# Weight panels fetched in pairs, and the quads of a fast matrix product regrouped for it

## The chip, the cores and the metric

The kernel runs on one core of a Trainium2 chip. A core has engines that work side by side, each through its own instructions in a fixed order: TensorE (PE, matrix products; PEld is its weight load), VectorE (DVE), ScalarE (ACT), GpSimd (POOL) and SyncE (SP), which here only issues DMA transfers. Engines wait for each other by semaphores. An instruction that waits holds up everything behind it on its engine. The metric is the device time of one execution, in microseconds (us).

## The reference

One step of a one-layer streaming encoder, in float32, for a prompt of 1024 rows and a sample of 64 rows, 1088 in all, with a model width of 1024. Cut to what matters:

```python
xn = rms_norm(x, g_pre)
z = xn @ w_in                    # 1024 -> 8208 columns, one projection for all that follows
xa, ga, q, k, v, gb, fl, ma, mb = jnp.split(z, np.cumsum(sizes)[:-1], axis=-1)
ua, conv_new = causal_conv(xa, conv_hist, conv_w, conv_b)
ya = rg_lru(ua, ...) * silu(ga)              # branch A, a gated linear recurrence
yb = fox_attention(q, k, v, logf) * silu(gb) # branch B, 16 heads of 64, causal, with forget gates
u = einsum('bsnw,nwd->bsnd', stack([ya, yb]), w_branch)
mix = sum(sigmoid(stack([ma, mb])) * u) @ w_o
h = x + rms_norm(mix, g_post)
h = h + rms_norm(sigmoid(h @ w_ple_gate) * (pe @ w_ple_proj), g_ple)
```

The keys, the values, the forget logits and the states are outputs too.

## The kernel before

Products keep float32 accuracy by splitting each operand into a high part (rounded) and a low part (what is left); three products, high x high, low x high and high x low, are summed. ScalarE writes the high part (`copy_act`, L82) and VectorE subtracts for the low part (`sub`, L85). So before a weight panel can be used, ScalarE reads it once ("wh") and VectorE once ("wl").

A *panel* is 128 columns of a weight matrix, 1024 x 128 numbers or 512 KB, in memory 1024 rows of 512 bytes. A plain panel takes 72 matmuls.

The stages, in order of time (us of the profile):

1. Norm and transposes of x, and the values v (to about 130), then two plain panels of a gate.
2. *Quads*, to about 431. A quad computes two panels at once by a fast product with seven instead of eight block products (`seven`). Each of the seven is 24 matmuls on one of three PSUM banks. Before the products, `split_pair` lets GpSimd form sums of the weight blocks (s1 to s4) and ScalarE and VectorE split them. While quad i runs, the weights of quad i + 1 are split and those of quad i + 2 fetched (`load_pair`). The eight first quads hold one key panel and one query panel each. Four others hold panels for branch A and for gates.
   Behind the products VectorE and ScalarE form sums of the banks (`u2`, `u3`, `p1`) and four results, by `put`: the first after the third product, then one each after the fifth, sixth and seventh. A key result is a tile "ko", a query result "qo", of which there are two buffers each. Results go to memory as a high part ("oh", by ScalarE's queue) and a low part ("kl" or "qo", by SP). Keys must also be transposed for the output: `keys_out` does this on TensorE ("tpk"), one item after each product (`between`), at the earliest three products after the result was made. A key buffer is free when the last of its items has run.
3. Attention, about 431 to 896. Its instruction order comes from a planner: the code runs through score, transpose and value steps in the order in which TensorE shall do them, counts their estimated durations (`spent`), and books the work of the other engines on a timetable (`book`, with costs as `D_MAX`, the row maximum on VectorE). Into this are mixed the matmuls of 18 plain panels (the gates), as `filler`, so that TensorE has work while the softmax runs. Loads of each head's q and k (`load_head`), the sample's data (`load_sample`) and the fillers' weights (`look_ahead`) are issued on SP in code order.
4. Branch A (to about 1068), the two products with w_branch ("a" to about 1182, "b" to about 1278), and the two last projections.

Weights for plain panels are fetched by `look_ahead` into two buffers of one panel each; `panel` and `book_split` split the next one while the present one is used. The order of instructions on each engine is fixed when the kernel is built; no engine picks another instruction when the first one waits.

Of the kernel before, what the change touches and what calls it, by code (L numbers as in the profile page):

```python
# [7 lines left out]
F32 = mybir.dt.float32  # L8
# [5 lines left out]
P = 128  # L14
D = 1024
KT = D // P
# [49 lines left out]
def hybrid_step(tc, a, o):  # L66
# [11 lines left out]
    def f(ap):  # L78
        return ap.bitcast(F32)

    def copy_act(out, in_, scale=1.0):
        act.activation(out=out, in_=in_, func=AF.Copy, scale=scale)  # L82

    def sub(eng, out, in0, in1):
        return eng.tensor_tensor(out=out, in0=in0, in1=in1, op=ALU.subtract)  # L85
# [106 lines left out]
    def chunk(steps):  # L192
        for _ in range(KT):
# [6 lines left out]


    wpool = sb("wpool", bufs=2)
    gates = deque([(w_in[:, c + k * P:c + (k + 1) * P], d[k]) for c, d in ((C_MA, d_ma), (C_MB, d_mb), (C_GB, d_gb))
                   for k in range(KT)])
    n_gates = len(gates)

    quads = [[(w_in[:, c + p * P:c + (p + 1) * P], (t, p)) for c, t in ((C_K, "k"), (C_Q, "q"))] for p in range(NP)]
    some = [(w_in[:, C_XA:C_XA + P], d_x0)]
    some += [(w_in[:, C_GA + k * P:C_GA + (k + 1) * P], d_ga[k]) for k in GA_EARLY]
    some += [gates.pop() for _ in range(2 * MORE)]  # L210
    quads += [[(src, ("r", dst)) for src, dst in some[i:i + 2]] for i in range(0, len(some), 2)]
# [5 lines left out]
    later = deque([(w_in[:, (C_XA if t == "x" else C_GA) + k * P:][:, :P], (t, k)) for t, k in branch_a]  # L217
                  + [(w_br[i * D:(i + 1) * D, k * P:(k + 1) * P], (t, k)) for i, t in enumerate("ab") for k in range(KT)])
    held_back = [True]
    ahead = deque()  # L220

    def choose():

        if held_back[0] and len(gates) <= n_gates - PLAIN:
            return None
        if gates:
            src, dst = gates.popleft()
            return src, ("r", dst)
        return later.popleft() if later else None

    def fetch(src, tag):
        raw = wpool.tile([P, KT, P], F32, name="wraw")
        tc.keep_in_program_order(sp.dma_start(raw[:, :, :], src.rearrange("(k p) n -> p k n", p=P)))
        ahead.append([tag, raw, None])

    def look_ahead():
        while len(ahead) < 2:
            nxt = choose()
            if nxt is None:
                return  # L240
            fetch(*nxt)

    def split_next(eng):
        if ahead and ahead[0][2] is None:
            raw = ahead[0][1]
            wh = wpool.tile([P, KT, P], F32R, name="wh")
            wl = wpool.tile([P, KT, P], F32R, name="wl")
            copy_act(wh[:, :, :], raw[:, :, :])
            sub(eng, wl[:, :, :], raw[:, :, :], f(wh[:, :, :]))
            ahead[0][2] = (wh, wl)  # L250

    def panel(eng=None):

        look_ahead()
        if not ahead:
            return None
        split_next(eng or dve)
        tag, _, w = ahead.popleft()
        look_ahead()
        split_next(eng or dve)  # L260
        return tag, w

    def spill(dst, t0, n, z):
# [37 lines left out]

    def load_wv(k):
        if k in (3, 4):
            raw = wpool.tile([P, KT, P], F32, name="wraw").rearrange("p k n -> p (k n)")
# [237 lines left out]

# [217 lines left out]

    def seven(i, w, ahead_, last):
        B11, B21, B22 = blk(0, 0), blk(1, 0), blk(1, 1)
        (_, d1), (_, d2) = quads[i]
# [24 lines left out]
        dve.tensor_tensor(out=u2, in0=zb, in1=p1, op=ALU.add)  # L788
# [10 lines left out]
        dve.tensor_tensor(out=u3, in0=zb, in1=p1, op=ALU.add)  # L799
# [122 lines left out]
    def book_split():  # L922

        if ahead and ahead[0][2] is None:
            raw = ahead[0][1]
            wh = wpool.tile([P, KT, P], F32R, name="wh")
            wl = wpool.tile([P, KT, P], F32R, name="wl")
            at = book("A", now[0] + 5000.0, A_W, lambda: copy_act(wh[:, :, :], raw[:, :, :]))
            book("D", at, D_W, lambda: sub(dve, wl[:, :, :], raw[:, :, :], f(wh[:, :, :])))
            ahead[0][2] = (wh, wl)  # L930

    def filler():
        left = deque()
        while True:
            look_ahead()
            if not ahead or ahead[0][0][0] != "r":
                return
            (_, dst), _, w = ahead.popleft()
            look_ahead()
            book_split()  # L940

            def evac(c, t0, n, z, dst=dst):
                def do():
                    spill(dst, t0, n, z)
                    left.popleft()

                left.append(book("A", now[0] + 497.0 + HOP_PE, A_ST, do))

            for _ in panel_steps(mm, *w, xs, evac):
                spent(497.0)  # L950
                if len(left) > 1:
                    catch_up(left[0])
                yield True
# [98 lines left out]
    def values(u, g, h, q2):  # L1052
# [5 lines left out]
        for j in range(2):  # L1058
            v = vv[:, 2 * g + j, :, :].rearrange("p s d -> p (s d)")
            half = j if g < q2 else 1 - j  # L1060
            c = slice(half * 256, (half + 1) * 256)
            pe.matmul(pv[:, :256], v, th[:, c], start=(g == 0 and j == 0), stop=False)  # L1062
# [524 lines left out]
    def quarter(pl, raws, src, q):  # L1587
        wh = pl.tile([P, KT, QW], F32R, name="wqh", tag="wqh")
        wl = pl.tile([P, KT, QW], F32R, name="wql", tag="wql")
        for i in range(2):  # L1590
            ks_ = slice(4 * i, 4 * i + 4)
            raw = raws.tile([P, KT, P], F32, name="wraw", tag="wraw", bufs=2).rearrange("p (k a) n -> p k (a n)", a=2)
# [7 lines left out]
    for of in range(KT):  # L1600
# [12 lines left out]
        tag, w = panel()  # L1613
        assert tag == ("b", of)
        if of == KT - 1:
            wo.append(quarter(wq0, wpool, a["w_o"], 0))
        run(panel_steps(mm, *w, yb, evac_b))
    p5.close()
    ybpool.close()
# [250 lines left out]
```

## Time and profile before

| what | us |
|---|---|
| median of 3 runs (1513.16 to 1516.97) | 1513.39 |
| the profiled execution | 1520.73 |
| its span, first to last instruction | 1519.0 |
| TensorE busy | 1460.3 |
| VectorE busy | 877.1 |
| ScalarE busy | 688.4 |
| GpSimd busy | 360.8 |

The mean granted clock of TensorE is 0.983 of full speed. The DMA queues take 38.2% (q1) and 4.8% (q10) of sixteen engines' time, and 182.82 MB move in all. In the rows below, a group row gives line, engine, operation, tiles; a timeline row gives start, length, engine, line, operation, `out<-in`, shape, a count, and in brackets how long the engine stood idle before it and what it had waited for. A row of the waits is: who waited, for whom, then the sum, how many times, and the longest. A row of the windows is: window, its length, busy time of the engine with its number of instructions, granted clock, share of the DMA engines, and GB/s.

### The profile page before, as it was taken

What the parts mean: (1) busy time and instruction counts of PE and PEld (TensorE: products, weight loads), DVE (VectorE), ACT (ScalarE), POOL (GpSimd) and SP (SyncE); (2) the same over time, 40 slices, a digit from 0 to 9 for tenths busy, and PEclk for the clock granted to TensorE, in tenths of its full rate; (3) what the DMA queues carried; (4) which work ended last, traced back from release to release, by engine and by line L of the source; (5) the groups of instructions that cost most, each with busy time, mean ns of one, the idle gap of its engine ahead of it and who ended that gap; (6) DMA issues with size and microseconds to landing.
All of it is one profiled execution on the core that took longest, in us unless ns stands there. A gap on an engine that the chain in (4) does not pass through costs nothing.

```text
span 1519.0 us, 26162 instructions
## 1 busy us (share of the span) xinstructions
PE 1460.3 (96%) x10096; PEld 1433.4 (94%) x10096; DVE 877.1 (58%) x1516; ACT 688.4 (45%) x1343; POOL 360.8 (24%) x443
## 2 busy tenths in 40 slices
PE   7999899999988999999999999989999999999997
PEld 7999899999987999999999999988999999999997
DVE  5464666653314666656556555999855544337644
ACT  4423344343114556556556545566544332324543
POOL 3011323313222332333233212546322000000001
PEclk8999999999998999999999999999999999999999
DMA  5354555554266554545645231211278544215111
GB/s 197 105 124 89 140 166 176 155 171 133 73 184 158 129 138 117 144 125 123 127 117 140 52 92 42 55 33 43 74 235 269 179 144 134 84 30 169 56 49 42
DMA packets 172696, 182.82 MB, mean 120 GB/s; under 512 B 21756, under 2 KB 143324, under 8 KB 172572
## 3 DMA queue, kind: packets, MB, share of 16 engines
q1 hardware_dynamic: 154908, 155.52, 38.2%
q10 hardware_dynamic: 17664, 25.64, 4.8%
q8 instruction: 79, 1.29, 0.4%
q14 instruction: 45, 0.37, 0.1%
HBM read 122.65 MB, written 58.46 MB: 119 GB/s over the span
## 4 chain that ended last, share of the span: by engine, by line
PE 71%; DVE 9%; DMA 9%; ACT 5%; issue 3%; POOL 2%; SPq 1%; ACTq 0%; DVEq 0%; POOLq 0%
PE quad L704 14%; PE acc L158 11%; PE acc L160 11%; PE acc L159 11%; PE tp L1038 4%; DMA wraw<-in_w_in 3%; PE pv L1062 2%; PE pv L1063 2%; PE s L1016 2%; PE s L1017 2%; DMA gb_in<-d_gb 1%; PE vacc L158 1%; PE vacc L159 1%; PE vacc L160 1%; DMA d_ma<-st 1%
## 5 line engine op out<-in xcount | busy, mean ns | idle before, releaser
L160 PE MATMUL acc<-xh,wl 128*128 128x364 f32 (+1 forms) x768 | 254.0, 331 | 6.8 <-DVE wl L85 6.8
L158 PE MATMUL acc<-xh,wh 128*128 128x364 f32 (+1 forms) x768 | 255.6, 333 | 0.0
L159 PE MATMUL acc<-xl,wh 128*128 128x364 f32 (+1 forms) x768 | 254.1, 331 | 0.0
L160 PEld LDWEIGHTS acc<-xh,wl 128*128 128x128 f32 x768 | 146.2, 190 | 7.4 <-DVE wl L85 7.4
L158 PEld LDWEIGHTS acc<-xh,wh 128*128 128x128 f32 x768 | 146.5, 191 | 1.1
L159 PEld LDWEIGHTS acc<-xl,wh 128*128 128x128 f32 x768 | 146.6, 191 | 0.7
L85 DVE TENSOR_TENSOR wl<-wraw,wh 128x1024 fp32r<-128x1024 f32 (+1 forms) x84 | 96.2, 1146 | 70.3 <-ACT wh L82 70.0
L82 ACT ACTIVATE wh<-wraw 128x1024 fp32r<-128x1024 f32 (+1 forms) x84 | 78.2, 931 | 93.0 <-PE quad L704 49.1
L996 DVE CUSTOM_DVE_ANT_0 s<-s,mask 128x128 f32<-128x128 f32 (+7 forms) x128 | 95.6, 768 | 24.9 <-PE s L1017 24.5
L1001 POOL TENSOR_SCALAR pb<-pb,sm 128x896 f32<-128x896 f32 (+1 forms) x64 | 61.8, 965 | 197.5 <-DVE sm L1000 175.9
L704 PE MATMUL quad<-xh,wh 128*128 128x272 f32 x384 | 82.3, 296 | 5.7 <-ACT p__1579 L82 4.7
L85 DVE TENSOR_TENSOR tl<-tp,th 128x512 fp32r<-128x512 f32 x96 | 65.5, 688 | 28.9 <-ACT th L82 28.8
L704 PE MATMUL quad<-xl,wh 128*128 128x272 f32 x384 | 80.0, 290 | 0.0
L1016 PE MATMUL s<-k,q 128*128 128x256 f32 (+1 forms) x192 | 68.1, 358 | 12.1 <-ACT pm L998 10.4
L704 PE MATMUL quad<-xh,wl 128*128 128x272 f32 x384 | 79.7, 289 | 0.0
L998 ACT ACTIVATE pb<-s,nm 128x896 f32<-128x896 f32 (+1 forms) x64 | 61.1, 955 | 35.7 <-DVE nm L996 27.5
L82 ACT ACTIVATE th<-tp 128x512 fp32r<-128x512 f32 x96 | 56.7, 597 | 37.3 <-PE tp L1038 34.1
L158 PE MATMUL acc<-wqh,hth 128*128 128x256 f32 x256 | 73.0, 285 | 0.0
L158 PE MATMUL acc<-wqh,mxh 128*128 128x256 f32 x256 | 72.5, 283 | 0.0
L159 PE MATMUL acc<-wql,mxh 128*128 128x256 f32 x256 | 72.4, 283 | 0.0
L160 PE MATMUL acc<-wqh,mxl 128*128 128x256 f32 x256 | 72.4, 283 | 0.0
L159 PE MATMUL acc<-wql,hth 128*128 128x256 f32 x256 | 72.4, 283 | 0.0
(527 smaller groups left out, 4255.8 us busy)
## 6 DMA issues: line engine op xcount, KB each, us to landing
wraw<-in_w_in SPq DMA_DIRECT2D x58, 512.0 KB
q<-d_q SPq DMA_DIRECT2D x48, 256.0 KB
k<-d_k SPq DMA_DIRECT2D x48, 256.0 KB
wraw<-in_w_branch SPq DMA_DIRECT2D x16, 512.0 KB
d_k<-oh ACTq DMA_DIRECT2D x16, 272.0 KB
d_k<-kl SPq DMA_DIRECT2D x16, 272.0 KB
d_q<-oh ACTq DMA_DIRECT2D x16, 272.0 KB
d_q<-qo SPq DMA_DIRECT2D x16, 272.0 KB
```

What stands on the lines that cost most here:

```text
L82: act.activation(out=out, in_=in_, func=AF.Copy, scale=scale)
L85: return eng.tensor_tensor(out=out, in0=in0, in1=in1, op=ALU.subtract)
L158: pe.matmul(out, ah, bh, start=start, stop=False)
L159: pe.matmul(out, ah, bl, start=False, stop=False)
L160: pe.matmul(out, al, bh, start=False, stop=stop)
L704: pe.matmul(acc[:, c, :CW], l[:, k, :], r[:, k, c * CW:(c + 1) * CW], start=(first and k == 0 and p == 0), stop=(k == 3 and p == 2), skip_ ...
L996: at = book("D", now[0] + HOP_PE, per(D_MAX, n), lambda: dve.tensor_tensor_reduce(out=s[:, :n], in0=s[:, :n], in1=m, scale=-1.0, scalar=-N ...
L998: free = book("A", at, per(A_EXP, n), lambda: act.activation(out=pr[:, :n], in_=s[:, :n], func=AF.Exp, scale=-1.0, bias=nm, accum_out=sm))
L1001: return free, book("G", at, per(G_NORM, n), lambda: pool.tensor_scalar(out=pr[:, :n], in0=pr[:, :n], scalar1=sm, scalar2=1.0, op0=ALU.mul ...
L1016: pe.matmul(s[:, c0:c0 + w], t["q1"][:, q0:q0 + P], t["k1"][:, c0:c0 + w], start=True, stop=False)
L1017: pe.matmul(s[:, c0:c0 + w], t["q2"][:HD + 4, q0:q0 + P], t["k2"][:HD + 4, c0:c0 + w], start=False, stop=True)
L1038: pe.transpose(tp[:, o0 + i * P:o0 + (i + 1) * P], pr[par][:, kb * P:(kb + 1) * P], ident[:, :])
```

## The change

1. Weights are fetched two neighbouring panels at a time, 1024 rows of 1 KiB, 1 MB in one DMA, into one buffer `w_raw`. Single panels (branch A, and four panels in quads) go to one half of it in turn.
2. The quads are regrouped so that the two panels of a quad are neighbours in memory: keys p and p + 1 in one quad, queries p and p + 1 in the next. Before it was key p with query p.
3. The next pair is requested when both panels of the present one are split. At the end of the quads both panels of a pair are split (`first_fill = panel()`), and the next pair is requested at that place, ahead of the loads of the first head.
4. The planner's cost for the row maximum is (310, 1.035) instead of (240, 1.05) (ns, and ns for each column). In the value products the low part `tl` goes ahead of the high part `th`.

The core of the diff:

```diff
-D_MAX, D_INV, D_LO, D_Y, D_YS = (240.0, 1.05), 160.0, (130.0, 1.1), 420.0, 230.0
+D_MAX, D_INV, D_LO, D_Y, D_YS = (310.0, 1.035), 160.0, (130.0, 1.1), 420.0, 230.0
...
-    quads = [[(w_in[:, c + p * P:c + (p + 1) * P], (t, p)) for c, t in ((C_K, "k"), (C_Q, "q"))] for p in range(NP)]
+    quads = [([cols(c + p * P)], ((t, p), (t, p + 1))) for p in range(0, NP, 2) for c, t in ((C_K, "k"), (C_Q, "q"))]
...
+    w_raw = wpool.tile([P, 2 * KT * P], F32, name="w_raw", bufs=1)
+    raw_pair = w_raw.rearrange("p (k n) -> p k n", k=KT)
+    raw_half = [w_raw[:, i * KT * P:(i + 1) * KT * P] for i in range(2)]
...
     def look_ahead():
+
         while len(ahead) < 2:
-            nxt = choose()
-            if nxt is None:
+            if held_back[0] and len(gates) <= n_gates - PLAIN // 2:
                 return
-            fetch(*nxt)
+            if not (gates or later):
+                return
+            src, tags = (gates or later)[0]
+            if any(not e[3] and max(len(tags), e[4]) > 1 for e in ahead):
+                return
+            (gates or later).popleft()
+            if len(tags) > 1:
+                dst = raw_pair
+                raws_ = panels(raw_pair)
+            else:
+                dst = raw_half[n_single[0] % 2].rearrange("p (k n) -> p k n", k=KT)
+                raws_ = [dst]
+                n_single[0] += 1
+            tc.keep_in_program_order(sp.dma_start(dst, src.rearrange("(k p) n -> p k n", p=P)))
...
     def load_pair(i):
-        pl = (wpool, sp_)[i % 2]
-        got = []
-        for src, _ in quads[i]:
-            raw = pl.tile([P, KT, P], F32, name="wraw", tag="wraw", bufs=2)
-            sp.dma_start(raw[:, :, :], src.rearrange("(k p) n -> p k n", p=P))
-            got.append(raw)
-        return got
+        raw = sp_.tile([P, KT, 2 * P], F32, name="wraw", tag="wraw", bufs=1)[:, :, :] if i % 2 else raw_pair
+        src = quads[i][0]
+        for dst, s in zip([raw] if len(src) == 1 else panels(raw), src):
+            sp.dma_start(dst, s.rearrange("(k p) n -> p k n", p=P))
+        return panels(raw)
...
-    split_next(dve)
+    first_fill = panel()
...
-            pe.matmul(pv[:, :256], v, th[:, c], start=(g == 0 and j == 0), stop=False)
-            pe.matmul(pv[:, :256], v, tl[:, c], start=False, stop=(g == q2 and j == 1))
+            pe.matmul(pv[:, :256], v, tl[:, c], start=(g == 0 and j == 0), stop=False)
+            pe.matmul(pv[:, :256], v, th[:, c], start=False, stop=(g == q2 and j == 1))
```

What it moves is seen best in the engines' instructions. VectorE around the end of quad 0, before (`ko_1817` is the fourth result of quad 0, made from the bank after the seventh product; `u2__1892` belongs to quad 1, `wl_1938` is a low split for quad 2):

```order
L734 TENSOR_TENSOR qo_1775<-quad_1588,p1__1579 128x544 [waits PE_49]
L85 TENSOR_TENSOR wl_1783<-s1_1581,wh_1782 128x512 [waits Activation_49]
L85 TENSOR_TENSOR wl_1783<-wraw_1545,wh_1782 128x512 [waits Activation_49]
L745 SCALAR_TENSOR_TENSOR qo_1775<-qo_1775,oh_1777 128x544 [waits Activation_49]
L734 TENSOR_TENSOR ko_1817<-quad_1615,u2__1613 128x544 [waits PE_49]
L85 TENSOR_TENSOR wl4_1826<-s4_1583,wh4_1825 128x512 [waits Activation_49]
L745 SCALAR_TENSOR_TENSOR kl_1822<-ko_1817,oh_1819 128x544 [waits DMAHW1_49,Activation_49]
L788 TENSOR_TENSOR u2__1892<-quad_1867,p1__1858 128x544 [waits PE_49,Activation_49]
L85 TENSOR_TENSOR wl_1938<-wraw_1550,wh_1937 128x1024 [waits DMAHW4_49,PE_49,Activation_49]
```

Now (all four results of quad 0 are keys; the fourth is `ko_1807`):

```order
L748 TENSOR_TENSOR ko_1764<-quad_1576,p1__1567 128x544 [waits PE_49]
L85 TENSOR_TENSOR wl4_1816<-s4_1571,wh4_1815 128x512 [waits Activation_49]
L759 SCALAR_TENSOR_TENSOR kl_1769<-ko_1764,oh_1766 128x544 [waits DMAHW6_49,Activation_49]
L748 TENSOR_TENSOR ko_1807<-quad_1603,u2__1601 128x544 [waits PE_49]
L85 TENSOR_TENSOR wl_1935<-w_raw_101,wh_1934 128x1024 [waits DMAHW2_49,Activation_49]
L802 TENSOR_TENSOR u2__1895<-quad_1865,p1__1856 128x544 [waits DVE_49]
```

The fourth key result, the low split of 1024 and u2 now stand in this order; before, u2 stood ahead of the split. TensorE in the same place now, from the transposes after the second product of quad 1 to its fourth product (some equal rows of the third product left out at its start):

```order
L727 MATMUL tpk_1890<-ident_76,ko_1721 96x128 [waits Activation_49]
L718 MATMUL quad_1821<-xh1_109,wh_1661 128x272 [waits Activation_49]
L718 MATMUL quad_1821<-xh1_109,wh_1661 128x272
L718 MATMUL quad_1821<-xl1_111,wh_1661 128x272 x2
L718 MATMUL quad_1821<-xh1_109,wl_1662 128x272 x2
...
L727 MATMUL tpk_1922<-ident_76,ko_1721 64x128 [waits PE_49,Activation_49]
L718 MATMUL quad_1865<-t3h_1304,wh8_1691 128x272 [waits DVE_49]
```

`ko_1721` is the second key result of quad 0. Its last transpose, `tpk_1922`, stands behind the third product of quad 1; the PE semaphore that `ko_1807` waits for is this transpose, since the two buffers of "ko" are taken by the second and third result. The product behind it, with t3h, waits for `u2__1895`. Before, at this place stood the product's own wait for a u2 that VectorE made from the bank of the second product.

SP at the start of attention, before:

```order
L736 DMA d_gb<-qo 128x544 x3
L916 DMA q_4795<-d_q 64x1024 x2
L916 DMA k_4797<-d_k 64x1024 x2
L916 DMA q_4796<-d_q 64x1024
L916 DMA k_4798<-d_k 64x1024
L917 DMA k_4798<-d_rows 4x1024
...
L988 DMA qsl<-d_q 64x64 x2
L233 DMA wraw<-in_w_in 128x8x128 x2
L916 DMA q_4994<-d_q 64x1024 x2
```

Now:

```order
L750 DMA d_gb<-qo 128x544 x3
L254 DMA w_raw<-in_w_in 128x8x256
L930 DMA q_4765<-d_q 64x1024 x2
L930 DMA k_4767<-d_k 64x1024 x2
L930 DMA q_4766<-d_q 64x1024
L930 DMA k_4768<-d_k 64x1024
L931 DMA k_4768<-d_rows 4x1024
```

The fillers' third and fourth panel, fetched behind the loads of head 0 and of the sample (qsl is the last of these) before, are now fetched as one pair ahead of them.

More of the change, by code (lines that the diff above doesn't have):

```diff
@@ L202, in hybrid_step, with panels, cols @@
     wpool = sb("wpool", bufs=2)
-    gates = deque([(w_in[:, c + k * P:c + (k + 1) * P], d[k]) for c, d in ((C_MA, d_ma), (C_MB, d_mb), (C_GB, d_gb))
-                   for k in range(KT)])
-    n_gates = len(gates)
-    quads = [[(w_in[:, c + p * P:c + (p + 1) * P], (t, p)) for c, t in ((C_K, "k"), (C_Q, "q"))] for p in range(NP)]
[L208 to L211, printed above, removed]
+    w_raw = wpool.tile([P, 2 * KT * P], F32, name="w_raw", bufs=1)
+    raw_pair = w_raw.rearrange("p (k n) -> p k n", k=KT)
+    raw_half = [w_raw[:, i * KT * P:(i + 1) * KT * P] for i in range(2)]
+    def panels(src):
+        return [src[..., i * P:(i + 1) * P] for i in range(2)]
+    def cols(c, n=2):
+        return w_in[:, c:c + n * P]
+    gates = deque((cols(c + k * P), (d[k], d[k + 1])) for c, d in ((C_MA, d_ma), (C_MB, d_mb), (C_GB, d_gb))
+                  for k in range(0, KT, 2))
+    quads = [([cols(c + p * P)], ((t, p), (t, p + 1))) for p in range(0, NP, 2) for c, t in ((C_K, "k"), (C_Q, "q"))]
+    some = [(cols(C_XA, 1), d_x0)] + [(cols(C_GA + k * P, 1), d_ga[k]) for k in GA_EARLY]
+    for (s1, d1), (s2, d2) in (some[:2], some[2:]):
+        quads.append(([s1, s2], (("r", d1), ("r", d2))))
+    for _ in range(MORE):
+        src, (d1, d2) = gates.pop()
+        quads.append(([src], (("r", d1), ("r", d2))))
     n_gates = len(gates)
@@ L216, in hybrid_step @@
         branch_a += [("g", k)] if k not in GA_EARLY else []
-    later = deque([(w_in[:, (C_XA if t == "x" else C_GA) + k * P:][:, :P], (t, k)) for t, k in branch_a]
-                  + [(w_br[i * D:(i + 1) * D, k * P:(k + 1) * P], (t, k)) for i, t in enumerate("ab") for k in range(KT)])
+    later = deque([(cols((C_XA if t == "x" else C_GA) + k * P, 1), ((t, k),)) for t, k in branch_a]
+                  + [(w_br[i * D:(i + 1) * D, k * P:(k + 2) * P], ((t, k), (t, k + 1)))
+                     for i, t in enumerate("ab") for k in range(0, KT, 2)])
     held_back = [True]
+    n_single = [0]
     ahead = deque()
[L222 to L234, printed above, removed]
     def look_ahead():
         while len(ahead) < 2:
-            nxt = choose()
-            if nxt is None:
+            if held_back[0] and len(gates) <= n_gates - PLAIN // 2:
                 return
-            fetch(*nxt)
+            if not (gates or later):
[12 more added lines that the diff above has]
+            tc.keep_in_program_order(sp.dma_start(dst, src.rearrange("(k p) n -> p k n", p=P)))
+            for tag, raw in zip(tags, raws_):
+                ahead.append([tag if isinstance(tag, tuple) else ("r", tag), raw, None, False, len(tags)])
     def split_next(eng):
@@ L257, in panel @@
         split_next(eng or dve)
-        tag, _, w = ahead.popleft()
+        tag, _, w, *_ = ahead.popleft()
         look_ahead()
         split_next(eng or dve)
+        look_ahead()
         return tag, w
@@ L303, in load_wv @@
         if k in (3, 4):
-            raw = wpool.tile([P, KT, P], F32, name="wraw").rearrange("p k n -> p (k n)")
+            raw = raw_half[k - 3]
         else:
@@ L762, in seven @@
         B11, B21, B22 = blk(0, 0), blk(1, 0), blk(1, 1)
-        (_, d1), (_, d2) = quads[i]
+        d1, d2 = quads[i][1]
         def more():
@@ L924, in book_split, with low @@
         if ahead and ahead[0][2] is None:
-            raw = ahead[0][1]
+            e = ahead[0]
+            raw = e[1]
             wh = wpool.tile([P, KT, P], F32R, name="wh")
             wl = wpool.tile([P, KT, P], F32R, name="wl")
-            at = book("A", now[0] + 5000.0, A_W, lambda: copy_act(wh[:, :, :], raw[:, :, :]))
-            book("D", at, D_W, lambda: sub(dve, wl[:, :, :], raw[:, :, :], f(wh[:, :, :])))
-            ahead[0][2] = (wh, wl)
+            e[2] = wh, wl
+            def low():
+                sub(dve, wl[:, :, :], raw, f(wh[:, :, :]))
+                e[3] = True
+                look_ahead()
+            at = book("A", now[0] + 5000.0, A_W, lambda: copy_act(wh[:, :, :], raw))
+            book("D", at, D_W, low)
     def filler():
         left = deque()
+        nxt = first_fill
         while True:
[L935 to L939, printed above, removed]
+            if nxt is None:
+                look_ahead()
+                if not ahead or ahead[0][0][0] != "r":
+                    return
+                nxt = ahead.popleft()[:3:2]
+            (_, dst), w = nxt
+            nxt = None
             book_split()
@@ L1615, in hybrid_step @@
         if of == KT - 1:
-            wo.append(quarter(wq0, wpool, a["w_o"], 0))
+            wo.append(quarter(wq0, raw_half, a["w_o"], 0))
         run(panel_steps(mm, *w, yb, evac_b))
```

9 lines of the change are left out of this document (5 added, 4 removed).

## The prediction

> **What bounds the kernel now.** I read the page first, then the view of waits for TensorE, the chain, the timelines of the places found so, and the view of windows for the granted clock.
>
> ```profile
> span 1519.0 us, 26162 instructions
> PE 1460.3 (96%) x10096; PEld 1433.4 (94%) x10096; DVE 877.1 (58%) x1516; ACT 688.4 (45%) x1343; POOL 360.8 (24%) x443
> ...
> PEclk8999999999998999999999999999999999999999
> ```
>
> TensorE is busy for 96% of the span, so time goes only where it waits, or where its clock is low. The change touches no matmul. I therefore count the waits that it takes away and those that it makes. The waits of before (sum, times, longest):
>
> ```profile
> PE s L1016 <- ACT pm L998: 10.4, 1, 10.4
> ...
> PE quad L704 <- ACT p__1579 L82: 4.7, 1, 4.7
> ...
> PE quad L704 <- DVE u__3463 L799: 2.5, 1, 2.5
> ...
> PE s L1016 <- ACT pb L998: 1.7, 1, 1.7
> ...
> PE pv L1062 <- DVE y L1071: 1.5, 1, 1.5
> ```
>
> The chain names the transfers behind several of them (start, length, what):
>
> ```profile
> 145.84 12.42 DMA d_ma<-st
> ...
> 300.39 11.42 DMA d_k<-kl
> ...
> 452.63 6.94 DMA wraw<-in_w_in
> ...
> 677.48 6.28 DMA wraw<-in_w_in
> 740.24 14.57 DMA wraw<-in_w_in
> ```
>
> A wait has a second price. The windows that begin at the end of a wait (length, TensorE busy, count, granted clock, DMA share, GB/s; the last two rows show transfers instead):
>
> ```profile
> 163.44:167.10 3.66, 3.65 (x17) 0.53 0.38 88
> 313.31:317.20 3.89, 3.89 (x19) 0.56 0.81 251
> ...
> 685.91:689.90 3.99, 3.99 (x26) 1.00 0.13 30
> 756.57:764.40 7.83, 7.83 (x30) 0.56 0.62 169
> ...
> 452.40:462.70 10.30, 0.00 (x0) 0.73 0.63 129
> ...
> 462.79:467.30 4.51, 4.51 (x16) 0.50 0.96 213
> ```
>
> After waits of 1.7, 2.5, 4.7 and 10.4 us the clock is near half; after 1.5 us it is full. The loss is 3.66 x 0.47 = 1.7, 3.89 x 0.44 = 1.7, 7.83 x 0.44 = 3.4 and 4.51 x 0.50 = 2.3 us. So a wait from about 1.7 us up costs some 1.7 us more than its length.
>
> **Step 1, the start of attention: -12.7, then +1.3.** Around the longest wait:
>
> ```profile
> 449.48 0.32 PE L160 MATMUL acc<-xh,wl 128*128 128x364 f32 x1
> 449.65 0.28 PE L1016 MATMUL s<-k,q 128*128 128x256 f32 x1
> ...
> 462.79 0.58 PE L1016 MATMUL s<-k,q 128*128 128x256 f32 x1 [10.43 <-ACT pm L998]
> ```
>
> ```profile
> 459.66 1.06 ACT L82 ACTIVATE wh<-wraw 128x1024 fp32r<-128x1024 f32 x1 [12.28 <-DMA wraw<-in_w_in]
> 462.27 0.37 ACT L998 ACTIVATE pm<-s,nm 128x128 f32<-128x128 f32 x1 [1.56 <-DVE nm L996]
> ```
>
> ScalarE stands 12.28 us before a weight panel that was requested only at 452.63 (chain), behind head 0's and the sample's loads. The first exponential is queued behind that split, and TensorE waits 10.43 us for it. In the changed kernel both panels of the last pair are split before attention, and the next pair is asked for ahead of head 0's loads. The split keeps its place before the exponential, but its data comes some 20 us earlier. Gain: 10.43 + 2.3 = 12.7 us.
>
> The price is that head 0's loads now queue behind 1 MB.
>
> ```profile
> 432.13 1.12 SPq L916 DMA_DIRECT2D q<-d_q  x2
> ```
>
> ```profile
> q<-d_q SPq DMA_DIRECT2D x48, 256.0 KB
> ```
>
> The pair and six loads of 256 KB are 2.62 MB from 432.1 on. At 213 GB/s (window above) they land 12.3 us later, at 444.4; at 129 GB/s 20.3 us later, at 452.4. The first score stands at 449.65. So the new wait is between nothing and 2.8 us, with the slow clock 4.5. I take +1.3, nearer to nothing: as many transfers are in flight here as in the 213 window.
>
> **Step 2, the rest of attention: -4.** Nine fetches of a pair replace eighteen of a panel, each asked for when the second panel's split is done, a whole panel (72 matmuls) before it is needed. The late ones of before:
>
> ```profile
> 755.25 0.28 ACT L82 ACTIVATE pts<-tps 128x128 f32<-128x128 f32 x1 [3.48 <-DMA wraw<-in_w_in]
> ```
>
> Here ScalarE is held 3.48 us by the panel of 740.24, and this makes the 1.7 us wait with its 3.4 us of slow clock; the panel of 677.48 stands before the 1.5 us wait. All gone would be -6.6. ScalarE's stores of spills can still be held by a weight transfer of 1 MB; one more case like 740.24 costs 5.1. I take -6.6 + 0.5 x 5.1 = -4, bounds -6.6 and +5.
>
> **Step 3, keys before queries: +20.3.** A quad computes two panels in seven products, every one of 24 matmuls. Before, each quad held a key panel and a query panel. Now quads of two key panels alternate with quads of two query panels. A key result ("ko") has two buffers and is freed only when its transposes, one piece after each product, are done. Two key results a quad fitted; four do not. The fourth waits for the last transpose of the second (64x128), which stands after the third product of the *next* quad. On VectorE behind the fourth result stand a low split (128x1024) and u2, and TensorE's next product waits for u2. The durations of before:
>
> ```profile
> 187.07 0.72 DVE L788 TENSOR_TENSOR u__1892<-quad,p__1858 128x544 f32<-128x544 f32 x1 [1.57 <-PE quad L704]
> 190.84 1.23 DVE L85 TENSOR_TENSOR wl<-wraw,wh 128x1024 fp32r<-128x1024 f32 x1 [3.04 <-ACT wh L82]
> 193.35 0.73 DVE L745 SCALAR_TENSOR_TENSOR kl<-ko,oh 128x544 f32<-128x544 f32 x1 [1.29 <-DMA d_k<-kl]
> ```
>
> ```profile
> 189.75 1.06 ACT L82 ACTIVATE wh<-wraw 128x1024 fp32r<-128x1024 f32 x1 [4.87 <-PE quad L704]
> ```
>
> ```profile
> 193.41 3.02 PE quad L704 x24
> ```
>
> The high split "wh" waits for the third product too. So from its end: wh 1.06, wl 1.23, u2 0.72 is 3.0, with the handovers 3.2 us; the fourth key result (0.72, as u2) lies beside wh. In before u2 ran ahead of wl, during the third product (3.02), and cost nothing. With the slow clock a transition costs 3.2 + 1.7 = 4.9 us, and there are four: 19.6. At the second one a kl of 0.73 is also ahead of u2: 20.3. Lower bound: wl not in the way, 0.72 + 0.72 = 1.4 us, below the 1.5 at which the clock stayed full: 5.8. Upper bound: at each the 1.29 + 0.73 of a kl that waits for its store: 27.8. I take 20.3, because the order of instructions on each engine is fixed.
>
> By the Trainium skill, "TensorE: Matmul & The Clock Gate", section "Why this matters for your kernels", the clock falls back after idle gaps of more than about 3 us, and the window in which this is judged runs free. By that rule 3.2 us would be at the edge, and the sum could be 6.8 lower; the rows above, half clock after 1.7 and 2.5 us, disagree, and the sum goes by them.
>
> **Step 4, other places where 1 MB must land at once: +1.5.** Panel A, used first after the quads, was ready with the first 512 KB; now it waits for both. In "a" and "b" of the branch stage the pair has one buffer, so the next request waits for the second panel's split.
>
> ```profile
> 410.01 1.12 SPq L233 DMA_DIRECT2D wraw<-in_w_in  x2
> ...
> 1121.36 0.49 SPq L233 DMA_DIRECT2D wraw<-in_w_branch  x1
> ```
>
> At 129 to 213 GB/s 1 MB takes 4.9 to 8.1 us, which a panel covers (72 matmuls at 0.17, the distance of the two starts at 449.48 and 449.65, are 12 us); at twice that, one wait of some 2 us with slow clock (3.7) at each of the two rows. Bounds 0 and +7.4; +1.5 as the low end is nearer.
>
> **Step 5, the first quads: 0.** The waits of 4.7 and 2.5 us, with 1.7 each of slow clock, hang on a store of 12.42 and one of 11.42 us that ran beside weight transfers. The pairs move these transfers, but the bytes stay. Both waits may go (-10.6), or one like the larger come (+6.4). Nothing in the trace tells which, so 0. The planner's new cost for the row maximum and the order of the two halves in the value products move single instructions; no wait of the list is on them: 0.
>
> **Sum:** -12.7 + 1.3 - 4 + 20.3 + 1.5 = +6.4 us on the profiled execution's 1520.73, so 1527.1. That execution lies 7.3 above the median of runs, 1513.39, which I attribute to nothing in the program; the difference carries over: 1519.8.
>
> **Rivals.**
> 1. *Faster:* at the transitions wl is already done, so only 1.4 us are waited and the clock stays full. Step 3 is 5.8, the sum -8.1, 1505.3. It decides at a wait of about 1.6 us. For it: at 190.84 wl started 3 us before its quad's next u. Against: the fixed order puts wl ahead of u2. Chance 0.15.
> 2. *The clock stays full through 3.2 us waits:* sum 6.4 - 6.8 = -0.4, 1513.0. Against: the 2.5 us row. Chance 0.15. (It is the rule of the Trainium skill named above; the trace disagrees.)
> 3. *1 MB lands late:* step 1 costs its 4.5 instead of 1.3, step 2 brings nothing, step 4 costs 3.7: sum 6.4 + 3.2 + 4 + 2.2 = +15.8, 1529.2. For it: the 14.57 us panel. Chance 0.15.
> 4. *The longer rows do nothing:* then weights land as before and steps 1 to 4 stand, since no term rests on faster transfers. By the Trainium skill, "DMA: Bandwidth & Descriptors", section "Specifications", 512 B already suffices for full rate; no view of before compares the two row lengths from the same weights. It changes step 5 only, and is inside the forecast.
>
> The forecast has 0.5, the unnamed rest 0.05. About 0.3% or 4.5 us is what a measurement of this kernel can tell from no change. The forecast's own spread (step 5 above all) puts 0.34 of its 0.5 above 1517.9, 0.14 within and 0.02 below 1508.9; rival 1 gives 0.14 faster and 0.01 within, rival 2 0.03 faster, 0.1 within and 0.02 slower, rival 3 all slower, the rest even. Together: faster 0.2, same 0.27, slower 0.53. The range of 1507 to 1530 leaves out the lower half of rival 1 and the upper part of rival 3.
>
> **What would show it.** Step 1: no 10 us wait at the first scores, the weight split there released without a transfer. Step 2: no ScalarE wait above 3 us for weights in attention. Step 3: four waits of TensorE for a "u" of VectorE, about 3 us, in the quads that follow key quads, each with some 3.7 us at half clock behind it. Step 4: a wait near the end of the quads or at the third panel of "a". The prediction is wrong if the four waits are missing or below 1.6 us, or if the attention gap has only moved to head 0's loads.

## The result and the profile after

| | before | changed |
|---|---|---|
| median of 9 runs, us | 1515.56 (1512.08 to 1517.70) | 1522.59 (1517.92 to 1527.66) |
| the profiled execution, us | 1520.73 | 1523.38 |

The changed kernel is slower by 7.0 us: ratio 1.0048, 95% interval 1.0031 to 1.0065. The two profiled executions differ by only 2.7 us, because the one of before lies 5.2 us above its median and the one of after 0.8. So the traces are compared by stage. Here and below a stage's length is read from the timeline of TensorE, as the distance between the first matmul of the stage and the first of the next. Only attention ends with the end of its own last matmul, ahead of the first "gacc" of branch A, so that a wait there counts to branch A. The branch products begin with the first "held":

| stage, us | before | changed | difference |
|---|---|---|---|
| up to the first quad | 152.6 | 153.9 | +1.3 |
| quads | 278.2 | 294.2 | +16.0 |
| first fillers, up to the first score | 18.9 | 20.3 | +1.4 |
| attention from the first score | 456.8 | 440.5 | -16.3 |
| branch A | 174.0 | 175.9 | +2.0 |
| branch products and the end | 438.6 | 436.8 | -1.8 |

The view of waits for TensorE after (who waited for whom: sum, times, longest):

```profile
PE quad L718 <- ACT p__1567 L82: 6.4, 1, 6.4
...
PE quad L718 <- DVE u__3649 L802: 4.5, 1, 4.5
...
PE quad L718 <- DVE u__2475 L802: 3.3, 1, 3.3
PE quad L718 <- DVE u__1895 L802: 3.0, 1, 3.0
PE quad L718 <- DVE u__3063 L802: 2.7, 1, 2.7
PE acc L158 <- ACT st L82: 2.3, 2, 1.2
...
PE s L1040 <- ACT pb L1022: 1.8, 1, 1.8
PE tp L1062 <- POOL pm L1025: 1.7, 1, 1.7
...
PE quad L718 <- DVE u__4647 L813: 0.8, 1, 0.8
...
PE s L1041 <- DMA q<-d_rows: 0.4, 1, 0.4
```

Against before, the 10.4 us wait at the first scores is gone, and four waits for a "u" are there, 13.5 us in all. The first of them on VectorE, ScalarE and TensorE:

```profile
193.82 0.72 DVE L748 TENSOR_TENSOR ko<-quad,u__1601 128x544 f32<-128x544 f32 x1 [6.26 <-PE tpk L727]
194.87 1.23 DVE L85 TENSOR_TENSOR wl<-w_raw,wh 128x1024 fp32r<-128x1024 f32 x1 [0.32 <-ACT wh L82]
196.01 0.72 DVE L802 TENSOR_TENSOR u__1895<-quad,p__1856 128x544 f32<-128x544 f32 x1
```

```profile
193.62 0.27 ACT L82 ACTIVATE kst<-tpk 96x128 f32<-96x128 f32 x1 [5.28 <-DMA out_k_prompt<-kst]
193.79 1.04 ACT L82 ACTIVATE wh<-w_raw 128x1024 fp32r<-128x1024 f32 x1
```

```profile
193.52 0.27 PE L727 MATMUL tpk<-ident,ko 128*64 128x128 f32 x1
196.78 0.52 PE L718 MATMUL quad<-t3h,wh 128*128 128x272 f32 x2 [3.00 <-DVE u__1895 L802]
197.14 0.41 PE L718 MATMUL quad<-t3l,wh 128*128 128x272 f32 x2
...
198.70 0.66 PE L718 MATMUL quad<-t3h,wh 128*128 128x272 f32 x2
```

Transpose, fourth key result, low split, u2, product: the row of events that was forecast. At the fourth transition ScalarE came later still:

```profile
344.89 0.27 ACT L82 ACTIVATE kst<-tpk 96x128 f32<-96x128 f32 x1 [6.81 <-DMA out_k_prompt<-kst]
```

These two lines on "kst" were not forecast. At the first transition ScalarE had itself stood 5.28 us before the store of an earlier key block, and came free just when the third product ended; at the fourth it was late by over 1 us. This is taken up below.

The windows behind the four waits and behind the two of attention (window, length, busy TensorE, granted clock, DMA share, GB/s):

```profile
196.78:200.70 3.92, 3.92 (x21) 0.65 0.75 282
247.63:251.50 3.87, 3.87 (x22) 0.70 0.64 229
296.87:300.80 3.93, 3.93 (x19) 0.57 0.68 142
348.05:352.00 3.95, 3.95 (x19) 0.57 0.74 282
...
478.20:482.20 4.00, 4.00 (x24) 1.00 1.00 261
771.38:776.00 4.62, 4.59 (x30) 1.00 0.59 142
```

The slow clock took 1.4 + 1.2 + 1.7 + 1.7 = 5.9 us more (length times what the clock lacks). The waits of 1.7 and 1.8 us in attention cost no clock. Branch A is longer for a small reason of its own: its first "gacc" waits 1.69 us with a clock of 0.60 over the 4 us behind it, where before it waited 0.91 us and the clock stayed at 1.00.

### The profile page after: what moved, and what is told of

It reads as the page before. It is cut to its first block, busy times and chain, and to the rows that moved or that the text cites. A ratio compares the mean times of both kernels' runs of the same rounds, so it can differ in the third digit from the quotient of the medians.

```text
span 1521.7 us, 26089 instructions
## 1 busy us (share of the span) xinstructions
PE 1459.8 (96%) x10096; PEld 1433.4 (94%) x10096; DVE 881.2 (58%) x1516; ACT 687.9 (45%) x1343; POOL 358.3 (24%) x443
## 3 DMA queue, kind: packets, MB, share of 16 engines
q1 hardware_dynamic: 125788, 155.52, 39.6%
## 4 chain that ended last, share of the span: by engine, by line
PE 74%; DVE 9%; DMA 7%; ACT 5%; issue 3%; POOL 2%; SPq 1%; ACTq 0%; DVEq 0%; POOLq 0%
PE quad L718 16%; PE acc L160 11%; PE acc L158 11%; PE acc L159 11%; PE tp L1062 4%; PE pv L1086 2%; PE pv L1087 2%; PE s L1040 2%; PE s L1041 2%; DMA d_ma<-st 2%; PE vacc L158 1%; PE vacc L159 1%; DMA out_k_prompt<-kst 1%; PE vacc L160 1%; DVE u L1330 1%
## 5 line engine op out<-in xcount | busy, mean ns | idle before, releaser
L85 DVE TENSOR_TENSOR wl<-w_raw,wh 128x1024 fp32r<-128x1024 f32 (+1 forms) x66 | 83.7, 1269 | 49.0 <-ACT wh L82 48.3
L1020 DVE CUSTOM_DVE_ANT_0 s<-s,mask 128x1024 f32<-128x1024 f32 (+7 forms) x128 | 95.5, 767 | 26.1 <-PE s L1041 25.7
L82 ACT ACTIVATE wh<-w_raw 128x1024 fp32r<-128x1024 f32 (+1 forms) x66 | 64.3, 975 | 53.6 <-PE quad L718 20.6
L160 PE MATMUL acc<-wqh,htl 128*128 128x256 f32 x256 | 72.4, 283 | 0.0
```

The source lines that it names most:

```text
L160: pe.matmul(out, al, bh, start=False, stop=stop)
L1020: at = book("D", now[0] + HOP_PE, per(D_MAX, n), lambda: dve.tensor_tensor_reduce(out=s[:, :n], in0=s[:, :n], in1=m, scale=-1.0, scalar=-N ...
```

## Experiments

Each was timed in alternation with the kernel before on the same chip; ratios are to that.

**1. Four buffers for key and query results together** (instead of two and two).

```diff
-        s = kqp.tile([P, HT], F32, name=tag, tag=tag, bufs=2)
+        s = kqp.tile([P, HT], F32, name=tag, tag="res", bufs=4)
```

> The changed kernel, with key and query results sharing four buffers instead of two and two (the same memory). My theory: the four waits for u2 in the quads after key quads (3.00, 3.25, 2.68, 4.52 us in the profile after) come from the fourth key result waiting for a buffer, so all four go, with the half clock behind them (1.4 + 1.2 + 1.7 + 1.7): 19.4 us less than the changed kernel, about 1503 us, and u2 stands ahead of the low split on VectorE again. Rival: the bursts of key stores and transposes hold ScalarE anyway, so the waits stay over 2 us each and the time above 1517. Second rival: only the waits count and the slow clock costs nothing: about 1509.

Measured: 1516.5 us, ratio 0.9996 (0.9977 to 1.0014). The gain over the changed kernel is 6 us and not 19, though VectorE's order is as expected, u2 ahead of the low split. Of the four waits the second and the fourth are nearly gone (0.5 and 0.4 us); the first is 3.5 and the third 1.2 us. The first one now, on VectorE and then ScalarE:

```profile
194.14 0.72 DVE L759 SCALAR_TENSOR_TENSOR kl<-ko,oh 128x544 f32<-128x544 f32 x1 [8.88 <-DMA d_k<-kl]
194.78 0.72 DVE L802 TENSOR_TENSOR u__1895<-quad,p__1856 128x544 f32<-128x544 f32 x1
```

```profile
194.62 0.27 ACT L82 ACTIVATE kst<-tpk 96x128 f32<-96x128 f32 x1 [8.05 <-DMA out_k_prompt<-kst]
```

Both engines stand 8 to 9 us before stores of key data, each of which has one buffer. With the result buffer out of the way, the low part "kl" is what u2 is queued behind. So the first rival has its share: behind the buffers lies a second limit, the landing of stores. One more wait appeared in this run, at the end of the quads, where the pair of 1 MB landed late (ScalarE 11.93 us before it, TensorE 3.6 us):

```profile
428.90 1.06 ACT L82 ACTIVATE wh<-w_raw 128x1024 fp32r<-128x1024 f32 x1 [11.93 <-DMA w_raw<-in_w_in]
```

So two things kept the gain at 6 us: the four waits fell only from 13.5 to 5.6 us, and this new one grew from 0.8 to 3.6, with a clock of 0.50 over the 3.9 us behind it.

**2. Key with query again, in the changed kernel.**

```diff
-    quads = [([cols(c + p * P)], ((t, p), (t, p + 1))) for p in range(0, NP, 2) for c, t in ((C_K, "k"), (C_Q, "q"))]
+    quads = [([cols(C_K + p * P, 1), cols(C_Q + p * P, 1)], (("k", p), ("q", p))) for p in range(NP)]
```

> The changed kernel, with quads of one key and one query panel as in the kernel before (fetched as single panels in rows of 512 B); pairs stay everywhere else. My theory: as with four buffers the four waits go, about 1503 us; the difference to the kernel before is then the start of attention alone, 12 us. Rival: the gain of attention belongs to the pairs of the quads or is an accident of the profiled execution: about 1515, as before.

Measured: 1517.25 us, ratio 1.0008 (0.999 to 1.0026), as the rival had it. But the rival's reason is not what the trace shows: attention is 15 us shorter than before, and the four waits are gone (two others of about 2 us for a "u" are there). Most of the time went at the first quad, in one wait:

```profile
PE quad L718 <- ACT p__1570 L82: 12.7, 1, 12.7
```

```profile
166.19 0.47 ACT L82 ACTIVATE st<-acc 128x360 f32<-128x360 f32 x1 [15.50 <-DMA d_ma<-st]
```

ScalarE stood 15.50 us before a store of a plain panel; in before it stood 7.46 us at this place, and the store took 12.42 us. Both panels of the odd quad's pair were requested just ahead of that store here, where before the first of them had been requested at 125.4.

**3. The regrouping alone, in the kernel before.**

```diff
-    quads = [[(w_in[:, c + p * P:c + (p + 1) * P], (t, p)) for c, t in ((C_K, "k"), (C_Q, "q"))] for p in range(NP)]
+    quads = [[(w_in[:, c + r * P:c + (r + 1) * P], (t, r)) for r in (p, p + 1)]
+             for p in range(0, NP, 2) for c, t in ((C_K, "k"), (C_Q, "q"))]
```

> The kernel before, with only the quads regrouped (two key panels, then two query panels, each panel still fetched by itself in rows of 512 B). My theory: four waits for u2 of 2.7 to 4.5 us and the slow clock behind them, and the 10.4 us wait at the start of attention stays: 19 us above before, about 1535. Rival: with weights in single transfers the low split is done earlier, waits of 1.5 us without slow clock: about 1521.

Measured: 1540.1 us, ratio 1.0153 (1.0135 to 1.0171), 24.4 us above before. The four waits are 6.0, 3.4, 2.7 and 4.6 us, and the wait at the first scores is there with 10.0. The regrouping is the loss. Quads take 299.9 us in this profile, 21.7 more than before.

**4. The second pair requested where the kernel before requests.**

```diff
+    hold = [False]
+
     def look_ahead():
 
-        while len(ahead) < 2:
+        while len(ahead) < 2 and not hold[0]:
...
+    hold[0] = True
     first_fill = panel()
...
     load_sample(0)
+    hold[0] = False
+    look_ahead()
     fill = filler()
```

> The changed kernel, with the second pair requested behind head 0's and the sample's loads, where the kernel before requests its third panel; both panels of the first pair are still split before attention. My theory: ScalarE stands before the weight split again and the first exponential behind it, a wait of some 10 us and 2 us of slow clock instead of the 3.3 us in small waits: about 10 us above the changed kernel, 1532. Rival: what took the wait away is that two panels are split ahead, not the request: 1522, as the changed kernel.

Measured: 1541.2 us, ratio 1.0168 (1.0148 to 1.0187), 18.6 us above the changed kernel; the rival falls. The wait is larger than before's:

```profile
PE s L1043 <- ACT pm L1025: 16.8, 1, 16.8
```

```profile
485.90 1.06 ACT L82 ACTIVATE wh<-w_raw 128x1024 fp32r<-128x1024 f32 x1 [18.69 <-DMA k<-d_k]
```

ScalarE stands 18.69 us before the split of the pair requested at 472.41. The profile puts the end of this wait down to a load of keys that was issued behind the pair, at 475.87, and took 10.02 us. When the pair itself had landed isn't shown, nor why the split had to wait for that load.

**5. Only the request moved, in the kernel before.**

```diff
-    split_next(dve)
+    first_fill = panel()
...
     def filler():
         left = deque()
+        nxt = first_fill
         while True:
-            look_ahead()
-            if not ahead or ahead[0][0][0] != "r":
-                return
-            (_, dst), _, w = ahead.popleft()
+            if nxt is None:
+                look_ahead()
+                if not ahead or ahead[0][0][0] != "r":
+                    return
+                nxt = ahead.popleft()[::2]
+            (_, dst), w = nxt
+            nxt = None
             look_ahead()
             book_split()
```

> The kernel before, with only the request moved: both panels that are there at the end of the quads are split before attention, and the third panel (512 B rows, by itself) is requested ahead of head 0's loads. My theory: the 10.4 us wait at the first scores and its slow clock go, to some 2 us of small waits: 10 to 13 us below before, about 1504. Rival: the gain in attention needs pairs (fewer, earlier fetches): less than 5 us below before.

Measured: 1503.0 us, ratio 0.9926 (0.9905 to 0.9948). This is step 1 by itself, and it beats both kernels. ScalarE at the first scores:

```profile
445.58 1.06 ACT L82 ACTIVATE wh<-wraw 128x1024 fp32r<-128x1024 f32 x1 [0.48 <-ACT st L82]
448.57 0.37 ACT L1002 ACTIVATE pm<-s,nm 128x128 f32<-128x128 f32 x1 [1.94 <-DVE nm L1000]
```

The split no longer waits for a transfer. In the profile attention is 440.9 us, about as long as in the changed kernel (440.5).

**6. The quads of before with the pairs of the changed kernel in attention.** As experiment 2, and for odd quads two buffers of one panel instead of one of a pair:

```diff
     def load_pair(i):
-        raw = sp_.tile([P, KT, 2 * P], F32, name="wraw", tag="wraw", bufs=1)[:, :, :] if i % 2 else raw_pair
...
+        if i % 2:
+            got = [sp_.tile([P, KT, P], F32, name="wraw", tag="wraw", bufs=2)[:, :, :] for _ in range(2)]
+        else:
+            got = panels(raw_pair)
```

> The changed kernel with the quads of the kernel before: a key and a query panel in each, fetched singly, and for odd quads two buffers of one panel instead of one of a pair. Pairs only for the plain panels. In the last experiment with keys beside queries the first quad waited 12.7 us, where before it waited 4.7, and I put that on the single buffer of the odd quads, which moves both of their first fetches to 145 us in front of a store that ScalarE waits for. My theory: with that wait back at about 5 us, quads as before and attention some 14 us shorter, about 1504. Rival: the wait has to do with the plain pair ahead of it, stays, and the time is 1515.

Measured: 1503.4 us, ratio 0.9927 (0.9903 to 0.9952). The first quad's wait is back at 4.1 us, as expected, and quads take 278.0 us and attention 440.6. Experiment 5, with single panels, is as fast: 1503.0. But the two differ in more than the pairs. Experiment 6 has the planner's new number and the new order of halves (the new plan, for short), experiment 5 the old ones, and single panels with the new plan take 1518.3 (experiment 12 below). So single panels reach the same time with the old plan, and with the new plan held equal the pairs are 15 us faster. No run here has pairs with the old plan and these quads.

**7. Pairs fetched by two transfers in rows of 512 B**, at the same places of the changed kernel.

```diff
-            tc.keep_in_program_order(sp.dma_start(dst, src.rearrange("(k p) n -> p k n", p=P)))
+            for r_, s_ in zip(raws_, panels(src) if len(tags) > 1 else [src]):
+                if len(tags) == 1:
+                    r_ = dst
+                tc.keep_in_program_order(sp.dma_start(r_, s_.rearrange("(k p) n -> p k n", p=P)))
...
-        for dst, s in zip([raw] if len(src) == 1 else panels(raw), src):
+        for dst, s in zip(panels(raw), panels(src[0]) if len(src) == 1 else src):
```

> The changed kernel, with each pair fetched by two transfers of one panel in rows of 512 B, at the same places. My theory: row length is worth nothing here that TensorE waits for: within 5 us of the changed kernel, 1522. Rival: half as many rows land sooner, so without them the stores behind them come later, the waits at the key quads grow, and the time is above 1528. Third: the first panel of each pair now lands earlier, and the time is below 1517.

Measured: 1547.8 us, ratio 1.0222 (1.0195 to 1.0249), 25 us above the changed kernel. My theory fell, by a wide margin. Quads take 305.1 us (294.2 changed) and attention 452.5 (440.5). Waits of TensorE, then ScalarE in the first transition and in attention:

```profile
PE s L1043 <- ACT pb L1025: 9.4, 2, 6.7
PE quad L721 <- ACT p__1571 L82: 9.4, 1, 9.4
...
PE quad L721 <- DVE u__1900 L805: 7.1, 1, 7.1
```

```profile
201.42 0.27 ACT L82 ACTIVATE kst<-tpk 96x128 f32<-96x128 f32 x1 [9.34 <-DMA out_k_prompt<-kst]
...
777.00 1.01 ACT L1025 ACTIVATE pb<-s,nm 128x896 f32<-128x896 f32 x1 [8.18 <-DMA w_raw<-in_w_in]
```

The same stores hold ScalarE, longer: 9.34 us where the profile of the changed kernel had 5.28 (5.6 to 8.4 in other runs with the same quads, table below). In attention a weight transfer holds it for 8.18 us. By the chain, the store of 13.54 us at the first quad after takes 16.51 here:

```profile
147.75 13.54 DMA d_ma<-st
```

```profile
148.75 16.51 DMA d_ma<-st
```

The edit changes the row length and the number of transfers together; which of the two counts was not tried. The packets themselves took no longer: those of queue q1 filled 37.5% of sixteen engines' span here (154908 packets) and 39.6% in the changed kernel (125788), with the same 155.52 MB.

**8 to 12. The planner's number and the order of the halves.** Experiment 8 puts both back in the changed kernel, 10 only the number, 11 only the order; 9 is the changed kernel once more, and 12 is the kernel of experiment 5 with both new.

```diff
-D_MAX, D_INV, D_LO, D_Y, D_YS = (310.0, 1.035), 160.0, (130.0, 1.1), 420.0, 230.0
+D_MAX, D_INV, D_LO, D_Y, D_YS = (240.0, 1.05), 160.0, (130.0, 1.1), 420.0, 230.0
...
-            pe.matmul(pv[:, :256], v, tl[:, c], start=(g == 0 and j == 0), stop=False)
-            pe.matmul(pv[:, :256], v, th[:, c], start=False, stop=(g == q2 and j == 1))
+            pe.matmul(pv[:, :256], v, th[:, c], start=(g == 0 and j == 0), stop=False)
+            pe.matmul(pv[:, :256], v, tl[:, c], start=False, stop=(g == q2 and j == 1))
```

> The changed kernel, with the old cost of the row maximum and the high part ahead of the low part in the value products. My theory: no wait depends on them: within 5 us of the changed kernel, 1522. Rival: part of the shorter attention stage (16 us in the profile) comes from them: attention over 3 us longer, above 1526.

> The changed kernel once more, beside the next three on the same chip. Theory that the last experiment (old plan, 7 us above) was a difference of runs: the four lie within 4 us of each other where they share the quads. Rival, that the plan is worth 7 us: this one is about 1522 and the two old halves together make 7 us more.

> The changed kernel with the old cost of the row maximum alone. If the plan is worth 7 us and by its costs: about 1529. If by the order of the value products, or not at all: 1522.

> The changed kernel with the high part first in the value products alone. If the order of the halves is worth 7 us: about 1529. If not: 1522.

> The kernel before with the request moved (the 1503 us version) and the new cost of the row maximum and the low part first. If the plan is worth 7 us by itself: about 1496. If it is worth nothing: 1503. If it helps only where pairs come: 1503.

| | us | ratio to before | 95% interval |
|---|---|---|---|
| 8: both old | 1529.8 | 1.0094 | 1.0067 to 1.0121 |
| 9: changed kernel again | 1521.9 | 1.0055 | 1.0035 to 1.0075 |
| 10: old number | 1531.4 | 1.0111 | 1.0077 to 1.0144 |
| 11: old order of halves | 1524.8 | 1.0060 | 1.0038 to 1.0082 |
| 12: experiment 5 with both new | 1518.3 | 1.0019 | 1.0003 to 1.0035 |

The order of the halves is worth nothing that shows. The two kernels with the old number (8 and 10) are 8 and 9.5 us slower than experiment 9, but their runs spread widely, over 1521.9 to 1534.0 and 1522.9 to 1539.3 us, and the profiled execution of 8 is the fastest of its six, that of 10 the slowest. In the profile of 10 attention is 6.5 us longer than in the changed kernel, and the quads are 8.7 us longer, although their instructions are the same and stand ahead of everything that the number can reorder. So it isn't shown that the number itself costs these microseconds. What grew in the quads is seen beside the other runs that have the same quads. The four waits of TensorE for "u", and how long ScalarE stood before the store of "kst" ahead of the first and the fourth, in us:

| run | "kst", first | first wait | second | third | "kst", fourth | fourth wait |
|---|---|---|---|---|---|---|
| changed | 5.28 | 3.0 | 3.3 | 2.7 | 6.81 | 4.5 |
| 9 | 5.57 | 3.3 | 3.3 | 2.8 | 6.37 | 4.1 |
| 11 | 5.69 | 3.4 | 3.3 | 2.7 | 6.23 | 3.9 |
| 8 | 6.80 | 4.5 | 3.3 | 2.7 | 8.01 | 5.7 |
| 10 | 8.44 | 6.2 | 3.3 | 2.7 | 8.89 | 6.6 |

The second and the third wait hardly change. The first and the fourth grow with ScalarE's wait for the store: the second limit, seen without any edit to the quads.

In the kernel of experiment 5 the new number and order together cost 15 us, and here the profile of 12 shows the place. Attention is 14 us longer than in experiment 5:

```profile
PE pv L1066 <- DVE y L1075: 8.9, 2, 4.6
```

```profile
720.43 0.33 ACTq L266 DMA_DIRECT2D d_mb<-st  x1
720.80 0.60 ACT L82 ACTIVATE th<-tp 128x512 fp32r<-128x512 f32 x1 [5.31 <-DMA wraw<-in_w_in]
```

A spill's store is issued only at 720.43, when a weight panel has landed, and the split "th" is queued behind it. That the new plan moved this store against the landing of the panel fits these rows, but why the store waits for that panel isn't shown, and number and order weren't tried apart here.

## Why the prediction was right

Forecast +6.4 us (1519.8 against 1513.39), measured +7.0 (1522.59 against 1515.56). That the two lie within 0.6 us is partly luck: the sum was worked out on the profiled execution of before, and the two profiled executions differ by only 2.7 us. The two large parts were right in sign and nearly in size: the start and the rest of attention were to give 15.4 us and gave 14.9 in the traces, and the four waits were to cost 20.3 us and cost 19.4. By its steps:

- **Step 1 (-12.7 + 1.3 = -11.4): right.** Waits at the first scores fell from 10.43 to 3.3 us (1.2 for ScalarE's store, 0.4 for head 0's rows, 1.7 for GpSimd; the clock stayed full). By itself the early request is worth 12.4 us (experiment 5); undone, it costs 18.6 (experiment 4). The new wait that I priced at 1.3 is the one of 0.4 us.
- **Step 2 (-4): the size fits, the reason only in part.** In the changed kernel one wait of 1.8 us with full clock was left in attention, of 6.6 us. But experiment 5, with single panels and the old plan, has as short an attention (440.9 against 440.5 us), so pairs aren't needed for it. With the new plan single panels have 454.9 us (experiment 12). So part of what the prediction gave to pairs hangs on the plan, which step 5 had put at 0 because no wait of before was on it.
- **Step 3 (+20.3): the size is right, the cause was half of it.** Four waits of 13.5 us with 5.9 of slow clock make 19.4; the quads grew by only 16.0, since some waits of before are gone (step 5). Regrouping alone costs 24.4 (experiment 3), and without it the quads are as long as before (experiment 6). The step's claim that the fourth key result waits for a buffer is what the trace shows. What it missed is a second limit at nearly the same length, the stores of key data that land late beside weight transfers. So four buffers took only 7.9 of the 13.5 us of waits away, and a new wait for a pair of 1 MB kept the whole gain at 6 us and not 19 (experiment 1). The fourth wait (4.5 us) was the longest because ScalarE stood 6.81 us before such a store. My upper bound had a wait for a store in it, the value taken had not (the bound adds up to 27.7, not 27.8). The waits of 2.7 and 3.3 us, which stay the same in all five runs of the table above, are the ones that the step's 3.2 us describes.
- **Step 4 (+1.5): 0 in this profile.** The wait at the end of the quads was 0.8 as before, and no new wait for weights came in the branch stage. In experiment 1 the one at the end of the quads did come, with 3.6 us; the bounds hold it.
- **Step 5 (0): both signs came.** The first quad's wait went from 4.7 to 6.4 us, with one of 1.1 ahead of it; the 2.5 us wait of before is gone, and the ones of 0.75 and 1.0 us too.
- **Rival 2, full clock after 3 us, fell**: all four waits of 2.7 to 4.5 us were followed by 0.57 to 0.70. **Rival 1** fell with the four waits. **Rival 3** did not come. **Rival 4**, that the longer rows do nothing, stays open: with two transfers in rows of 512 B for each pair the changed kernel is 25 us slower (experiment 7), but row length and number of transfers changed together. Either way it does not touch the sum, since the sum took before's stores and waits as they were.

## What to carry to other kernels

Price a change of grouping by the buffers whose release stands in another group's work: an in-order engine turns one late release into a wait of every instruction behind it. When bytes are moved in larger pieces, look at the small stores that run beside them, and at engines that have only one buffer for such a store. When several edits come in one change, try each by itself: here the few lines that ask for weights earlier, alone, give 1503.0 us, and the regrouping around them turns that gain into a loss. And when a plan is changed, time it with each fetch scheme: single panels took 1503.0 us with the old plan and 1518.3 with the new.

## What the runs showed of the hardware that I had not expected

- The clock does not fall at one length of wait: 1.7 us before cost 3.4 us of half clock (756.57 in before), 1.7 and 1.8 us after cost nothing, and after 3.0 us TensorE still ran about 1 us at full clock (0.41 for two matmuls at 197.14) before it slowed (0.66 at 198.70). The Trainium skill, "TensorE: Matmul & The Clock Gate", section "Part 1: The HAM clock gate", says that the window in which activity is judged runs free. The trace fits that, though where in a window each wait fell can't be read from it; it doesn't fit one limit of length.
- Small stores land late beside weight transfers: one took 13.54 us in the changed kernel and 16.51 in experiment 7, where the chain of before has such a store with 2.25 us at 447.41. The Trainium skill, "DMA: Bandwidth & Descriptors", section "Specifications", gives 512 B as enough for full rate. The trace agrees as far as it goes: the packets of q1 took 37.5% of sixteen engines' span with the weight pairs in rows of 512 B and 39.6% in rows of 1 KiB. So no slower packets show behind the 25 us of experiment 7, and what they are due to stays open.
